# The eviction of a gate table from PSUM, walked in another order

## The chip, the cores and the metric

The kernel runs on one core of a Trainium2 chip. The metric is the device time of one execution in microseconds (us), the median of three runs. The core has five engines that run side by side, each in its own program order: TensorE (PE in the rows; PEld are its weight loads), VectorE (DVE), ScalarE (ACT), GpSimd (POOL) and SyncE (SP), which issues most transfers. Matmuls write to PSUM, a memory of eight banks with 512 float32 for each of 128 partitions; VectorE and ScalarE take results out of it ("evict" them) to SBUF, the large on-chip memory.

## What is computed

The reference is a trunk of two layers over 512 tokens of width 1024: attention heads of four kinds, then a layer of 16,384 small experts of which each token picks 128 (16 for each of 8 heads). The change lies in that second part:

```
def peer_ffn(h, w_q, sub_k1, sub_k2, u, v):
    q = (hf @ w_q).reshape(t, PEER_HEADS, 2, PEER_QUERY_DIM // 2)
    ...
    eid = jnp.take_along_axis(cid, top_j, axis=-1)
    gate = jax.nn.softmax(top_s, axis=-1)
    ...
        act = jax.nn.gelu(jnp.einsum('cd,ced->ce', hc, u[ec]).astype(jnp.float32))
        w = (gc * act).astype(hc.dtype)
        return jnp.einsum('ce,ced->cd', w, v[ec])
```

An expert's number is 128 times its first half plus its second half, two numbers below 128.

## The kernel before

Tokens lie in four tiles of 128. For three of them (384 tokens) the kernel doesn't gather experts but multiplies with all of them: 128 blocks of 128 experts go through TensorE, first with `u` (`u_mm`, line 1381, whose result `u_act` puts through gelu into `act`), later with `v`. Between the two each block's `act` is multiplied with the gates, which are zero for experts that a token didn't pick. For that a **gate table** is built in each layer, one gate for each token and each of the 16,384 experts. The fourth tile's tokens gather their experts with indirect transfers by GpSimd.

The table is built from pairs of one-hot rows, eight tokens (a "block" `b`) at a time, 48 blocks in a layer:

- `g_ones` (line 1657, VectorE) writes the one-hot rows of both halves of the expert numbers, tile `o`.
- `g_scale` (line 1664) multiplies those of the first half with the gates, in a high and a low part, tile `og`: the high part on VectorE (line 1675), the low part on VectorE or as eight small instructions on ScalarE (line 1673).
- `g_mm` (line 1677) multiplies them on TensorE. A bank of PSUM then holds four tokens of 128 second halves each, `(t a)` in its columns, with the first halves on the partitions. Each bank takes eight matmuls of 128 columns.
- `g_out` (line 1685) evicts that bank on ScalarE into the staging tile `gs`, `[128, 128, TG]`, whose last axis holds the tokens of a group of `TG` = 32: in `gs` the 128 second halves of one token lie 32 floats (128 bytes) apart, and neighbouring tokens lie next to each other. Four tokens fill 4 of the 32 places, eight evictions fill a tile.
- `g_put` (line 1691, SyncE) writes a full `gs` tile, 2 MB, to `gdram` in DRAM. There are 12 in a layer, and two `gs` tiles.

Later `gq_load` (line 1828) reads four blocks of experts at a time back, `w_mul` multiplies them into `act`, and `w_split` feeds the products with `v`.

The order of the work is set when the kernel is built, by the class `Plan` (line 100): it takes pieces of work with rough lengths and due times and lists them, and each engine runs its list in that order. For the eviction it reckons with 0.49 us on ScalarE (line 1724), for the scaling with 0.602 on VectorE or 2.4 on ScalarE, for the one-hot rows with 1.135. The first products with `u` are put between the pieces of the table (lines 1737 to 1749); the last four of those that go ahead are held until the table's last matmul is out. Buffers: three of `o`, two of `og`, six banks of PSUM.

The names in the rows below: `o<-iota,iT` are the one-hot rows, `og<-o,gT` and `og<-o,gL` the scaling on VectorE and on ScalarE, `psa<-og,o` the matmuls of the table, `gs<-psa` the eviction, `psb<-bh,uh` (and two more) the products with `u`, `gq<-gdram` the table's way back. The fourth token tile's expert numbers (`oh`, `pr`, `cid`, `ts`) are worked out on VectorE meanwhile.

Of the kernel before, what the change touches and what calls it, by code (L numbers as in the profile page):

```python
# [16 lines left out]
AF = mybir.ActivationFunctionType  # L17
# [25 lines left out]
GSC = 2.0 ** 14  # L43
# [12 lines left out]
# the chunks of w_in: for each run of columns the size of the rotated heads, the tile, the place in it, the width  # L56
# [22 lines left out]
def pairs(n):  # L79
    """the runs (first row, rows, columns) of pairs of ranks that can be among the n largest sums"""  # L80
    runs = []
    for k in range(n):
        w = n // (k + 1)
        if runs and runs[-1][2] == w:
            runs[-1][1] += 1
        else:
            runs.append([k, 1, w])
    return runs
# [11 lines left out]
class Plan:  # L100
    """an order for pieces of work, from rough lengths: each starts as soon as its inputs, buffers and engine allow, the most urgent first"""
# [28 lines left out]
    def holds(self, eng):  # L130
        """what a piece of work holds: its engine, and the way to SBUF that vector operations on two tiles (W) share with Pool"""
        return {"W": ("V", "port"), "G": ("G", "port") if LOCK else ("G",)}.get(eng, (eng,))
# [19 lines left out]
def trunk(ctx: ExitStack, tc: tile.TileContext, I, out):  # L152
    nc = tc.nc
    V, S, G, PE, SY = nc.vector, nc.scalar, nc.gpsimd, nc.tensor, nc.sync
# [79 lines left out]
    def ada_sum(j, acc, c):  # L234
        """sums over the rows, down the partitions or along the free axis"""
        ps = bank("b")
        if j in COL:
            for c in range(KD):
                PE.matmul(ps[:, c:c + 1], lhsT=acc[:, c * 128:(c + 1) * 128], rhs=ones[:, 0:1], start=True, stop=True)
        else:  # L240
            PE.matmul(ps[0:1], lhsT=ones[:, 0:1], rhs=acc[:, c * 512:(c + 1) * 512], start=True, stop=True)
        return ps
# [34 lines left out]
    def norm_cols(l, which):  # L277
        """the scale and the shift of a norm, once they are asked for"""
        g = small.tile([128, KD], F32, name="ng", bufs=2)
        SY.dma_start(g, I["norm_g"][l, which])  # L280
        got = []

        def cols():
            if not got:
                m = mods[l]
                gs = small.tile([128, KD], F32, name="ngs", bufs=2)
                V.scalar_tensor_tensor(gs, m["col"][:, 2 * which + 1], 1.0, g, op0=ALU.add, op1=ALU.mult)
                got.extend((gs, m["col"][:, 2 * which]))
            return got
        return cols  # L290

    def norm_parts(x, cols, pool, put, tag, nv=NV):
        """normed and modulated rows of one token tile, transposed, four chunks at a time: four steps"""
        xn = pool.tile([128, D], F32, name="xn", tag="xn", bufs=2)
        ps = {}

        ss = small.tile([128, 1], F32, name="nss")

        def squares():
            S.activation(xn, x, AF.Square, accum_out=ss)  # L300

        def scaled():
            rs = small.tile([128, 1], F32, name="nrs")
            rsqrt_mean(rs, ss, D)
            V.tensor_scalar(xn, x, rs, None, op0=ALU.mult)

        def turn(half):
            ps[half] = bank(tag)
            for k in range(4):
                PE.transpose(ps[half][:, k * 128:(k + 1) * 128], xn[:, (4 * half + k) * 128:(4 * half + k + 1) * 128], ident)  # L310

        def modulated(half):
            gs, sh = cols()
            h = pool.tile([128, 4, 128], F32, name="hf", tag="hf", bufs=3)
            for k in range(4):
                c = 4 * half + k
                if k < 4 - nv:
                    S.activation(h[:, k], ps[half][:, k * 128:(k + 1) * 128], AF.Identity, scale=gs[:, c:c + 1], bias=sh[:, c:c + 1])
                else:
                    V.tensor_scalar(h[:, k], ps[half][:, k * 128:(k + 1) * 128], gs[:, c:c + 1], sh[:, c:c + 1], op0=ALU.mult, op1=ALU.add)  # L320
            put(half, h)
        return squares, scaled, turn, modulated
# [39 lines left out]
    def rows_out(l):  # L362
        """what is done with each tile of rows that leaves layer l - 1"""
        if l == L:
# [19 lines left out]
            def halves(i, x, pool):  # L384
                """the same for a tile of rows that comes in two halves"""
# [28 lines left out]
    def early_mc(nat_):  # L414
        """the place of the first chunk's columns until the tiles they lie in are needed"""
        flat = {q: nat_[q].rearrange("p a b c -> p (a b c)") for q in ("dq", "dk")}
        return [flat["dq"][:, 384 * i:384 * i + 384] for i in range(3)] + [flat["dk"][:, :384]]

    def first_chunk(nat_, hh, hl):
        """the products with the first chunk of w_in, for a tile of rows and some of the inner blocks"""  # L420
        ps = {}

        def part(i, ks, wh, wl):
            if ks[0] == 0:
                ps[i] = bank("a")
            tsl = slice(i * 128, (i + 1) * 128)
            for k in ks:
                mm3(ps[i][:, :384], hh[:, k, tsl], hl[:, k, tsl], wh[:, k], wl[:, k], k == 0, k == KD - 1)
            if ks[-1] == KD - 1:
                S.activation(early_mc(nat_)[i], ps[i][:, :384], AF.Copy)  # L430
        return part

    class Room:
        """a pool over parts of tiles that nothing else needs yet"""
# [8 lines left out]
    def begin(O, RST, tp, more, hh, hl):  # L443
        """the modulation of the first norm, and what is done around the first chunk of w_in"""
# [39 lines left out]
    def w_in_phase(l, raw_, hh, hl, tp, pa, RST, O):  # L484
        """the products with w_in; what the heads need is made ready behind the chunk that follows"""
# [5 lines left out]
        def stack(dst, lo, hi, src, key):  # L491
            """one head transposed twice; the lower copy of a query, or a third and a fourth of a key, reduced to what float32r leaves"""
# [162 lines left out]
    for l in range(L):  # L655
        lam_init = 0.8 - 0.6 * math.exp(-0.3 * l)
        rcm, hcm, nat, hh, hl = state
        with tc.tile_pool(name=f"O{l}", bufs=1) as po_:
            O = po_.tile([128, KD, T], F32, name="O")
            # attention sub-layer  # L660
# [107 lines left out]
        # expert sub-layer  # L768
# [6 lines left out]
def attention(ctx, nc, tc, I, l, lam_init, st, O, RST, tp, small, bank, rope, nhalf, ca, ident, blk, rcm, right, ada):  # L775
# [20 lines left out]
    # differential lambda  # L796
# [18 lines left out]
    # NSA gates  # L815
# [22 lines left out]
    class Group:  # L838
        """four maps of one tile of tokens: scores, exponentials with the maximum taken off, sums, weights, sums of the values"""
# [56 lines left out]
        def plan(self, ready, before=None):  # L896
            """all of it; what the sums of the values go on from, if they do, is before"""
# [266 lines left out]
    def diff_prep(d, side, step, eng=None):  # L1164
        """differential queries of four maps one below the other, each with zeros in the place of the others, and the keys"""
# [26 lines left out]
    def mla_up(i, step):  # L1192
        """queries, keys and values of the latent heads"""
# [56 lines left out]
    # NSA  # L1250
# [59 lines left out]
    # more of the modulation  # L1310
# [45 lines left out]
def peer(nc, tc, I, l, xd, fh, fl, h3, closing, q0, w012, both, wq_mm, right, hp, up, small, bank, mm3, iota128, pos, ident, dram, grow, ada, more, rows_out):  # L1356
# [7 lines left out]
    # experts whose first product is kept in DRAM until the second one  # L1364
# [28 lines left out]
    with tc.tile_pool(name=f"Q{l}", bufs=1) as qp:  # L1393
# [25 lines left out]
        def wq_part(h, half, eng):  # L1419
            """one of the two parts of four blocks of rows of a head's w_q"""  # L1420
# [14 lines left out]
        def wq_late(h, c):  # L1435
            """the second half of the rows of the first two heads"""
            wq_mm(q0[2 * h + c], w[h], c, slice(256, 512), fh, fl)
# [10 lines left out]
        def key_mm(h, i):  # L1448
            """scores of the keys of one head"""
# [8 lines left out]
        def top16(rows, n):  # L1458
            """the 16 largest of each row and their places, with the rows in turn"""
# [12 lines left out]
        def key_best(h, i):  # L1472
            """the 16 largest of either half"""
# [13 lines left out]
        def pick(h):  # L1487
            """the sums of the 16 largest of the halves that can be among the 16 largest"""
# [9 lines left out]
        # the products with w_q and the best keys of each head  # L1498
# [5 lines left out]
        for h in range(8):  # L1504
# [25 lines left out]
            for i in range(NT):  # L1530
                # the rows that come late last
# [15 lines left out]
        def turn_over():  # L1547
            """the room of w_q goes to the sums of the first experts and to the gate table"""
# [19 lines left out]
        if True:  # L1568
# [9 lines left out]
            def ids(i, q, eng):  # L1578
                """numbers of the experts of the candidates for four slots of each head"""
# [55 lines left out]
            def turn(i):  # L1635
                """the halves of the expert numbers and the gates, slots on the partitions"""
# [20 lines left out]
            def g_ones(b):  # L1657
                """one-hot rows of the halves of the expert numbers of eight tokens"""
# [5 lines left out]
            def g_scale(b, q, eng):  # L1664
                """the first of them times the gates, in two parts"""
# [19 lines left out]
            def g_out(j):  # L1685
# [3 lines left out]
                S.activation(gst[tg][:, :, 4 * t4:4 * t4 + 4].rearrange("p a t -> p t a"), gps.pop(j).rearrange("p (t a) -> p t a", t=4), AF.Copy, scale=1 / GSC)  # L1689
# [4 lines left out]
            # the numbers and gates of the experts  # L1694
# [19 lines left out]
            # the gate table  # L1714
# [13 lines left out]
            # what can be done ahead of the sums over all experts  # L1728
# [77 lines left out]
    def g_weights():  # L1806
        """gate weights of the next eight slots, once a few later dot products are behind them"""
# [11 lines left out]
    with tc.tile_pool(name=f"D{l}", bufs=1) as dp, ExitStack() as order:  # L1819
# [57 lines left out]
        # made ready for the last products and for what follows them: what the steps before leave room for  # L1877
# [78 lines left out]
        with tc.tile_pool(name=f"X{l}", bufs=1) as xp:  # L1956
# [26 lines left out]
            # a tile of rows at a time, so that what follows can start on the first  # L1983
# [161 lines left out]
```

## Time and profile before

| | |
|---|---|
| time, median of 3 runs | 3389.96 us (3385.28 to 3396.86) |
| profiled execution, span from first to last instruction | 3387.4 us |
| TensorE busy | 3202.0 us, 95% |
| VectorE busy | 2593.0 us, 77% |
| ScalarE busy | 1542.2 us, 46% |
| evictions of the gate table (line 1689) | 192, 194.9 us |
| mean granted TensorE clock | 0.964 of full |

Busy time is the time in which an engine works on an instruction; neighbouring instructions of one engine overlap at their ends, so the step from one start to the next can be shorter than one instruction lasts. An average over the span says little: a layer has stages with different limits, and the windows below cut the building of the table out of it. The chain of work that ended last is followed back from the last instruction, at each step to what released it.

### The profile page before, as it was taken

The numbers are of one execution on the slowest core, as the hardware profiler recorded it, in microseconds if no ns is written. First come the engines' busy times: TensorE is split into PE (matmuls) and PEld (weight loads), VectorE is DVE, ScalarE is ACT, GpSimd is POOL, SyncE is SP. The second block draws the span as 40 slices with busy tenths as digits, with TensorE's granted clock in tenths as the row PEclk, the third lists the DMA queues.
The fourth block names the chain that finished last, engine by engine and source line by source line (L and its number), as shares of the span: only waits on it lengthen the run. The fifth ranks groups of instructions, "written<-read, shape, count | busy, mean of one in ns | idle before, by whom it ended". The sixth has DMA issues, their size and how long they took to land.

```text
span 3387.4 us, 48323 instructions
## 1 busy us (share of the span) xinstructions
PE 3202.0 (95%) x17540; PEld 2820.4 (83%) x17540; DVE 2593.0 (77%) x5460; ACT 1542.2 (46%) x2799; POOL 988.0 (29%) x756
## 2 busy tenths in 40 slices
PE   6988999979999999999999889999799999999998
PEld 6955879968989999998898568798699899999987
DVE  6487699867878888786665877988587788777766
ACT  3376526883333333333344764278633333333333
POOL 1254120003434343341023532100143344444400
PEclk9988999979999999999998999998799999999999
DMA  6223404458989998896632233044588899999954
GB/s 219 66 92 101 158 26 144 174 210 313 346 308 339 337 335 328 326 351 231 200 117 74 90 125 139 28 154 180 221 320 326 315 341 325 324 324 325 323 186 166
DMA packets 291342, 762.76 MB, mean 225 GB/s; under 512 B 23832, under 2 KB 130968, under 8 KB 285984
## 3 DMA queue, kind: packets, MB, share of 16 engines
q1 hardware_dynamic: 217376, 491.22, 42.0%
q0 software_dynamic: 73728, 268.47, 21.5%
q8 instruction: 137, 2.24, 0.3%
q14 instruction: 101, 0.83, 0.1%
HBM read 700.86 MB, written 58.74 MB: 224 GB/s over the span
## 4 chain that ended last, share of the span: by engine, by line
PE 76%; DVE 13%; ACT 6%; DMA 2%; issue 1%; POOL 0%; SPq 0%; DVEq 0%; POOLq 0%; ACTq 0%
PE psa L204 13%; PE psa L205 13%; PE psa L203 13%; PE psb L203 9%; PE psb L205 9%; PE psb L204 9%; ACT gs L1689 3%; PE psa L1683 2%; PE psa L851 2%; ACT og L1673 2%; DMA gq<-gdram 1%; PE psa L884 1%; DVE s L1466 1%; DVE ki L1464 1%; DVE ki L1470 1%
## 5 line engine op out<-in xcount | busy, mean ns | idle before, releaser
L203 PE MATMUL psb<-bh,uh 128*128 128x384 f32 x2048 | 692.0, 338 | 3.4 <-ACT act L1392 2.8
L205 PE MATMUL psb<-bh,ul 128*128 128x384 f32 x2048 | 688.7, 336 | 3.1 <-DVE ul L1379 3.1
L204 PE MATMUL psb<-bl,uh 128*128 128x384 f32 x2048 | 687.2, 336 | 0.0
L203 PE MATMUL psa<-vh,wdh 128*128 128x512 f32 x1512 | 590.3, 390 | 17.2 <-ACT wdh L1844 17.2
L205 PE MATMUL psa<-vh,wdl 128*128 128x512 f32 x1512 | 593.5, 393 | 0.0
L204 PE MATMUL psa<-vl,wdh 128*128 128x512 f32 x1512 | 593.3, 392 | 0.0
L1779 POOL DMA_INDIRECT gt<-in_peer_u,eid x256 | 338.2, 1321 | 727.9 <-DVE gt L1799 234.8
L1844 ACT ACTIVATE wdh<-act 128x384 fp32r<-128x384 f32 x252 | 132.1, 524 | 866.2 <-PE psa L204 637.3
L1779 POOL DMA_INDIRECT gt<-in_peer_v,eid x256 | 323.0, 1262 | 426.5 <-DVE a L1804 197.9
L203 PEld LDWEIGHTS psb<-bh,uh 128*128 128x128 f32 x2048 | 386.4, 189 | 13.8 <-ACT act L1392 4.0
L204 PEld LDWEIGHTS psb<-bl,uh 128*128 128x128 f32 x2048 | 385.9, 188 | 7.3
L205 PEld LDWEIGHTS psb<-bh,ul 128*128 128x128 f32 x2048 | 385.3, 188 | 4.8 <-DVE ul L1379 4.4
L1379 DVE TENSOR_TENSOR ul<-ur,uh 128x1024 fp32r<-128x1024 f32 x246 | 301.6, 1226 | 98.4 <-ACT uh L1376 84.9
L1845 DVE TENSOR_TENSOR wdl<-act,wdh 128x384 fp32r<-128x384 f32 x252 | 140.9, 559 | 285.4 <-ACT wdh L1844 274.5
L203 PEld LDWEIGHTS psa<-vh,wdh 128*128 128x128 f32 x1512 | 285.0, 189 | 73.0 <-ACT wdh L1844 17.8
L205 PEld LDWEIGHTS psa<-vh,wdl 128*128 128x128 f32 x1512 | 284.8, 188 | 60.0
L1856 DVE TENSOR_TENSOR vl<-vr,vh 128x1024 fp32r<-128x1024 f32 x252 | 307.7, 1221 | 34.1 <-ACT vh L1853 22.8
L204 PEld LDWEIGHTS psa<-vl,wdh 128*128 128x128 f32 x1512 | 284.8, 188 | 55.8
L1804 DVE SCALAR_TENSOR_TENSOR a<-gt,w,a 128x1024 f32<-128x1024 f32 x254 | 325.5, 1282 | 0.8
L1799 DVE SCALAR_TENSOR_TENSOR gt<-gt,h 128x1024 f32<-128x1024 f32 x256 | 310.8, 1220 | 0.0
L1376 ACT ACTIVATE uh<-ur 128x1024 fp32r<-128x1024 f32 x256 | 268.5, 1049 | 75.4 <-PE psb L204 63.6
L1392 ACT ACTIVATE act<-psb 128x384 f32<-128x384 f32 x256 | 126.8, 495 | 334.6 <-PE psb L205 334.5
(386 smaller groups left out, 5565.5 us busy)
## 6 DMA issues: line engine op xcount, KB each, us to landing
ur<-in_peer_uT SPq DMA_DIRECT2D x256, 512.0 KB
vr<-in_peer_v SPq DMA_DIRECT2D x256, 512.0 KB
gdram<-gs SPq DMA_DIRECT2D x24, 2048.0 KB
gq<-gdram SPq DMA_DIRECT2D x64, 768.0 KB
aw<-in_ada_w SPq DMA_DIRECT2D x58, 512.0 KB
gt<-in_ada_w SPq DMA_DIRECT2D x32, 512.0 KB
wr<-in_w_q SPq DMA_DIRECT2D x14, 1024.0 KB
wr<-in_w_out SPq DMA_DIRECT2D x16, 512.0 KB
```

Source lines behind the costliest of these rows:

```text
L203: PE.matmul(ps, lhsT=wh, rhs=mh, start=first, stop=False)
L204: PE.matmul(ps, lhsT=wh, rhs=ml, start=False, stop=False)
L205: PE.matmul(ps, lhsT=wl, rhs=mh, start=False, stop=last)
L1376: S.activation(uspl[e][0], uraw[e], AF.Copy)
L1379: eng.tensor_sub(uspl[e][1], uraw.pop(e), uspl[e][0])
L1392: S.activation(acts[e], ups.pop(e)[:, :384], AF.Gelu_apprx_tanh)
L1779: G.indirect_dma_start(out=t, out_offset=None, in_=I["peer_u" if kind == "u" else "peer_v"], in_offset=bass.IndirectOffsetOnAxis(ap=eid3[: ...
L1799: V.scalar_tensor_tensor(t, t, 1.0, h3, op0=ALU.mult, op1=ALU.mult, accum_out=d3[:, s:s + 1])
L1804: V.scalar_tensor_tensor(a3, t, w3[:, s:s + 1], a3, op0=ALU.mult, op1=ALU.add)
L1844: S.activation(wh, w, AF.Copy)
L1845: V.tensor_sub(wl, w, wh)
L1856: V.tensor_sub(vspl[e][1], vraw.pop(e), vspl[e][0])
```

## The change

One line of `g_out` is written in another way. The instruction stays one ACTIVATE on ScalarE that copies 128 x 512 float32 with a scale. Before, both sides were walked token by token (`p t a`): 128 second halves of a token, then the next token. Now both are walked second half by second half (`p a t`): the four tokens of one second half, then the next second half. The numbers and the places that they go to are the same. (The rest of the diff drops comments and docstrings.)

```
-                S.activation(gst[tg][:, :, 4 * t4:4 * t4 + 4].rearrange("p a t -> p t a"), gps.pop(j).rearrange("p (t a) -> p t a", t=4), AF.Copy, scale=1 / GSC)
+                S.activation(gst[tg][:, :, 4 * t4:4 * t4 + 4], gps.pop(j).rearrange("p (t a) -> p a t", t=4), AF.Copy, scale=1 / GSC)
```

`Plan` is told the same 0.49 us as before, so every engine's list keeps its order; on ScalarE the rows of the eviction alone read differently. This is the piece of ScalarE's list at the end of the first layer's table, the last three scalings on ScalarE (`og`) and the evictions (`gs`) around them:

```order
-L1673 ACTIVATE og<-o,gL 128x128 x8
-L1689 ACTIVATE gs<-psa 128x4x128 x4
-L1673 ACTIVATE og<-o,gL 128x128 x8
-L1689 ACTIVATE gs<-psa 128x4x128
-L1673 ACTIVATE og<-o,gL 128x128 x8
-L1689 ACTIVATE gs<-psa 128x4x128 x7
```

```order
+L1673 ACTIVATE og<-o,gL 128x128 x8
+L1689 ACTIVATE gs<-psa 128x128x4 x4
+L1673 ACTIVATE og<-o,gL 128x128 x8
+L1689 ACTIVATE gs<-psa 128x128x4
+L1673 ACTIVATE og<-o,gL 128x128 x8
+L1689 ACTIVATE gs<-psa 128x128x4 x7
```

Nothing moved: the same rows stand in the same places, with the eviction's free axes as 128x4 instead of 4x128.

## Rows read from the trace of the kernel before

**Rows 1.** The page, part 4: chain that ended last, by engine, by line.

```profile
PE 76%; DVE 13%; ACT 6%; DMA 2%; issue 1%; POOL 0%; SPq 0%; DVEq 0%; POOLq 0%; ACTq 0%
PE psa L204 13%; PE psa L205 13%; PE psa L203 13%; PE psb L203 9%; PE psb L205 9%; PE psb L204 9%; ACT gs L1689 3%; PE psa L1683 2%; PE psa L851 2%; ACT og L1673 2%; DMA gq<-gdram 1%; PE psa L884 1%; DVE s L1466 1%; DVE ki L1464 1%; DVE ki L1470 1%
```

**Rows 2.** Windows: length; PE, PEld, DVE, ACT, POOL busy (count); clock, DMA share, GB/s.

```profile
567.00:580.00 13.00, 11.91 (x85) 11.21 (x83) 11.35 (x14) 13.00 (x27) 0.00 (x0) 1.00 0.52 202
580.00:655.00 75.00, 75.00 (x504) 72.77 (x503) 63.36 (x112) 65.05 (x114) 5.75 (x2) 1.00 0.52 190
667.14:679.40 12.26, 8.99 (x64) 7.31 (x64) 11.33 (x15) 12.26 (x26) 0.00 (x0) 0.64 0.44 171
679.40:728.38 48.98, 35.28 (x256) 29.30 (x256) 39.20 (x61) 48.98 (x97) 0.00 (x0) 0.59 0.41 172
728.38:741.06 12.68, 11.25 (x73) 9.91 (x73) 6.87 (x17) 12.68 (x26) 0.00 (x0) 0.73 0.40 167
741.06:767.50 26.44, 17.02 (x96) 16.06 (x94) 5.37 (x5) 5.02 (x7) 6.84 (x6) 0.93 0.96 353
...
2354.60:2403.64 49.04, 35.30 (x256) 29.31 (x256) 39.20 (x61) 49.04 (x97) 0.00 (x0) 0.62 0.41 172
```

**Rows 3.** The same, of line 1689 alone: length, ACT busy (count), clock, DMA.

```profile
580.00:655.00 75.00, 28.33 (x27) 1.00 0.52 190
```

**Rows 4.** Timeline, one cycle: start, length, engine, group, [idle before, releaser].

```profile
703.80 0.69 DVE L1675 TENSOR_TENSOR og<-o,gT 128x1024 f16<-128x1024 f16 x1
703.86 2.66 ACT L1673 ACTIVATE og<-o,gL 128x128 f16<-128x128 f16 x8
704.40 0.78 DVE L1584 TENSOR_TENSOR cid<-ifl 128x128 int16<-128x128 int16 x7
704.44 4.41 PE L1683 MATMUL psa<-og,o 128*128 128x128 f16 x32 [1.70 <-ACT og L1673]
705.10 0.69 DVE L1675 TENSOR_TENSOR og<-o,gT 128x1024 f16<-128x1024 f16 x1
706.26 3.92 ACT L1689 ACTIVATE gs<-psa 128x512 f32<-128x512 f32 x4
706.88 0.69 DVE L1675 TENSOR_TENSOR og<-o,gT 128x1024 f16<-128x1024 f16 x1 [1.10 <-PE psa L1683]
707.49 2.52 DVE L1661 TENSOR_TENSOR o<-iota,iT 128x2048 f16<-128x2048 f16 x2
709.99 2.66 ACT L1673 ACTIVATE og<-o,gL 128x128 f16<-128x128 f16 x8
```

**Rows 5.** Groups by line and shape: count, busy us, mean ns, idle before.

```profile
L1689 ACT ACTIVATE gs<-psa 128x512 f32<-128x512 f32 x192 | 194.9, 1142 | 7.7 <-PE psa L1683 6.3
L790 ACT ACTIVATE PT<-psa 128x512 f32<-128x512 f32 x64 | 36.6, 591 | 17.5 <-PE psa L884 17.3
L1646 DVE CAST iT<-psa 128x256 f16<-128x256 f32 x6 | 2.5, 418 | 0.0
L792 DVE COPY PT<-psa 128x256 f32<-128x256 f32 x4 | 1.7, 422 | 0.0
L565 DVE TENSOR_TENSOR x<-x,posk 128x992 f32<-128x992 f32 x2 | 3.7, 1871 | 0.0
L1379 DVE TENSOR_TENSOR ul<-ur,uh 128x1024 fp32r<-128x1024 f32 x246 | 301.6, 1226 | 98.4 <-ACT uh L1376 84.9 <-issue 13.3
```

**Rows 6.** Timeline, three straight evictions on ScalarE in a row.

```profile
222.46 1.55 ACT L790 ACTIVATE PT<-psa 128x512 f32<-128x512 f32 x3
```

**Rows 7.** Timeline, the end of the first layer's table.

```profile
732.34 4.30 PE L1683 MATMUL psa<-og,o 128*128 128x128 f16 x31 [0.84 <-ACT og L1673]
734.16 6.87 ACT L1689 ACTIVATE gs<-psa 128x512 f32<-128x512 f32 x7
```

**Rows 8.** The chain that ended last, what follows it: start, length, what.

```profile
741.06 7.25 DMA gdram<-gs
749.71 17.20 DMA gq<-gdram
```

## The prediction

> **What bounds the kernel now.** I read the chain of work that ended last first: TensorE holds 76% of it, yet the eviction at line 1689 has 3% of its own and the scaling at line 1673 another 2% [rows 1]. Of some 3387 us, 5% is 170 us in which ScalarE, not TensorE, sets the pace. The windows by stage show where. While the first expert products are mixed in (580 to 655 us), TensorE is busy for 75.00 of 75.00 us and ScalarE for 65.05: there ScalarE hides. From 667.14 to 728.38 us it is the other way round: ScalarE is busy for 12.26 of 12.26 and 48.98 of 48.98 us, VectorE for 11.33 + 39.20, TensorE for 8.99 + 35.28 [rows 2]. The second layer repeats it [rows 2]. Matmuls are idle there and the granted clock falls to 0.59 of full speed, near the lower level of 1.2 GHz, for lack of work and not as a cause.
>
> The timeline shows what ScalarE does in it: a cycle of eight scalings and four evictions [rows 4]. From 703.86 to 706.26 (2.40 us) the scalings of an odd block run, from 706.26 to 709.99 (3.73 us) four evictions: 6.13 us a cycle, with no gap. TensorE works 4.41 us of it and waits 1.70 for ScalarE; VectorE waits 1.10 for TensorE. So an eviction costs 0.93 us of the path in this stage, although one lasts 1142 ns (neighbours overlap).
>
> **The one edit: what an eviction costs afterwards.** It stays one instruction of 128x512; there are 96 in each layer, in the same place on every queue, so no wait is added and nothing is moved past another queue. What changes is the walk. Before, PSUM is read straight through and each element is written 128 bytes from the last one in SBUF. Afterwards four neighbouring elements (16 bytes) are written in a run and then 128 bytes are hopped, but each element is read 512 bytes from the last one in PSUM.
>
> What the write costs is in the trace: the same 128x512 from PSUM, straight on both sides, lasts 591 ns against 1142 [rows 5], and three in a row take 1.55 us, a step of (1.55 - 0.59) / 2 = 0.48 us [rows 6]. So the scattered write doubles the eviction. That runs of four are enough to lose the penalty is shown on VectorE: the copy at line 1646 writes runs of four halves out of PSUM and lasts 418 ns for 256 columns, the straight copy 422 [rows 5].
>
> What the scattered read from PSUM costs no row shows. Every read of PSUM in this kernel is straight. Lower bound: nothing, a step of 0.48 us. A gain below that has no source, since 0.48 us is already the straight copy. Upper bound: a read on VectorE, from SBUF, with 64 bytes between elements lasts 1871 ns for 992 elements, where a straight one lasts 1226 for 1024 [rows 5]: 1.89 - 1.20 = 0.69 ns an element, 0.35 us for 512. Added to an eviction that kept its whole write penalty that is 1.49 us, a step of 1.28. I take the lower end: the row with scattered reads is of the other memory and another engine, and the only accesses to PSUM in the trace keep ScalarE's full pace. This is the weakest step, and the rivals below hang on it.
>
> The Trainium skill (Advanced Engine Details and Errata, section Memory Cachelines) says that SBUF wants two hits in each 16-byte line for full speed and PSUM two in each 8-byte line, and that patterns that aren't contiguous there slow matmuls. Its SBUF half agrees with 1142 against 591 ns; its PSUM half, read onto an eviction, speaks against the change, since each read would open a line of its own, and the eviction would stay near 1142 ns and the time near 3390 us. No run here shows that half.
>
> **The long stretch, 667.14 to 728.38 us.** It is ten cycles long (two irregular, eight regular): 61.24 us. ScalarE alone would now need 2.40 + 4 x 0.48 = 4.32 us a cycle. What is late next is VectorE. Its busy time over the stretch is 11.33 + 39.20 = 50.53 us, 5.05 a cycle [rows 2], in order: two one-hot tiles, three scalings, and a piece of the last token tile's expert numbers [rows 4]. Its wait for TensorE goes, I reckon: the scaling that waits needs the products of the odd block before. TensorE needs 4.41 us for both blocks, and VectorE comes to that scaling 5.05 us after the last one, so the products are done some 0.6 us earlier. I take VectorE's busy time and 0.5 us for joints: 51 us, a saving of 10.2 us. As ScalarE isn't the bound any more, this term needs only an eviction step under (5.05 - 2.40) / 4 = 0.66 us, not 0.48.
>
> **The end of the table, 728.38 to 741.06 us.** The last products end at 732.34 + 4.30 = 736.64 us; ScalarE has seven evictions standing then and ends at 734.16 + 6.87 = 741.03 [rows 7]. With steps of 0.48 it keeps up with the products and ends one eviction after them, near 736.64 + 0.1 + 0.6 = 737.3: a saving of 3.7 us. On it hangs the last write of the table to DRAM (7.25 us) and the first read back (17.20 us) [rows 8], which start when the last eviction ends; the loads around them are released by the same work. TensorE is busy for 17.02 of the 26.44 us from there to the first product that needs the table [rows 2], so there is room for them to come 3.7 us sooner: 9.4 us idle.
>
> **The front.** Between 567 and 580 us ScalarE is full (13.00 of 13.00) and TensorE idles 1.09 us [rows 2]: I count 1 us. From 580 to 655 nothing: TensorE is the cover. Were it gone, the 27 evictions in it [rows 3] would count too. In the short stretch from 655 to 667 I count 0.5 us, an estimate from the three evictions that stand before its last scaling (3 x 0.45 = 1.35), most of which TensorE's products hide.
>
> **The sum.** A layer: 10.2 + 3.7 + 1 + 0.5 = 15.4 us; both: 30.8. The loop over the experts that follows waits for nothing else and starts that much sooner. The profiled execution has a span of 3387.4 us, 2.6 below the median of 3389.96; so 3356.6 for the span and about 3359 for the median: 0.9% faster. About 0.3% (10 us) is what a measurement of this kernel can tell from no change.
>
> **Rivals.**
> *The penalty only changes sides.* One access in each pair is still scattered, now the read. If a scattered read of PSUM holds ScalarE as a scattered write to SBUF does, the step stays 0.93, the cycle 6.13, the time 3390 us. For it: the hop grows from 128 to 512 bytes, and [rows 5] has a scattered read that costs on VectorE. Against it: that is SBUF. 15%.
> *A part of it.* With a step of 0.75 us ScalarE stays the bound: 2.40 + 3.00 = 5.40 a cycle, a saving of 7.3 us over ten, and 7 x 0.18 = 1.3 at the end, 0.7 in front: 9.3 a layer, 3371 us. 8%.
> *Slower: the read costs more than the write did.* ScalarE has no slack in the long stretch, so it turns slower from the first nanosecond that a step is over 0.93. At the upper bound of 1.28 us: 40 evictions x 0.35 = 14 us there, 7 x 0.35 = 2.5 at the end. In the covered stretch 65.05 + 27 x 0.35 = 74.5 of 75 us still hides [rows 2, 3]; of the 20 or so other evictions (7 us) I count 4.5, since ScalarE is already full from 567 to 580. 21 us a layer, 3432 us. Against it: both bounds must be at their worst together. 9%.
> *The saving stops at VectorE.* If its own waits for TensorE don't shrink, the cycle is 5.05 + 1.10 = 6.15 and only the end is won: 5.2 us a layer, 3380 us. For it: it is the fuller of the two remaining engines. Against it: the wait is for products that themselves wait 1.70 us for ScalarE. Two cycles in between can fall to 4.4 us, TensorE's own need. 4%.
>
> **How the numbers follow.** My forecast 64%, a part 8%, stops at VectorE 4%, the same 15%, slower 9%. Faster by over 0.3%: 64 + 8 and half of the 4 = 74%; within 0.3%: 15 + 2 = 17%; slower 9%. The forecast alone is 3351 to 3368: 17 us a layer if all joints vanish, 13.5 if a cycle is 5.3, and 5 us for the scatter (three runs lie between 3385.28 and 3396.86). Eight in ten needs the unchanged case too, so the range is 3351 to 3394; it leaves out the slower case and a little beside.
>
> **What would show it.** The group of line 1689 with about 600 ns instead of 1142: the read is free. Near 1142: the first rival. In the long stretch ScalarE is no longer full, VectorE is over 95% busy and a cycle takes about 5.1 us. The last eviction of each layer ends within 1 us of the last product of the table, and the write to DRAM starts 15 us sooner in the first layer and 31 in the second. The stretch from 580 to 655 us keeps its length. Wrong would be a shorter eviction with cycles still at 6.1 us, or a gain that the loop over the experts gives back.

## The result, and the profile after

The changed kernel takes 3354.86 us (median of 4 runs, 3348.74 to 3358.83). The kernel before, run beside it, took 3392.47 us. The ratio is 0.9898, with a 95% interval from 0.9877 to 0.9919: about 1.0% faster. The forecast was 3359 us, in a range from 3351 to 3394. The profiled execution spans 3356.9 us, against 3387.4 before: 30.5 us less, where the sum of the prediction had 30.8.

First the page of the changed kernel, part 1 (busy time, share of the span, instructions), and part 4 (the chain of work that ended last), to be laid beside [rows 1]:

```profile
PE 3196.3 (95%) x17540; PEld 2823.5 (84%) x17540; DVE 2588.2 (77%) x5460; ACT 1468.2 (44%) x2799; POOL 990.0 (29%) x756
...
PE 79%; DVE 16%; DMA 2%; ACT 2%; issue 1%; POOL 0%; SPq 0%; DVEq 0%; POOLq 0%; ACTq 0%
PE psa L204 13%; PE psa L205 13%; PE psa L203 13%; PE psb L203 10%; PE psb L205 10%; PE psb L204 10%; PE psa L1683 4%; PE psa L851 2%; PE psa L884 1%; DVE o L1661 1%; DMA gq<-gdram 1%; DVE s L1466 1%; DVE og L1675 1%; DVE ki L1464 1%; DVE ki L1470 1%
```

ScalarE did as many instructions as before in 74.0 us less (1468.2 against 1542.2). The eviction at line 1689, 3% of the chain before, is gone from it, and so is ScalarE's scaling at line 1673; VectorE's share rose from 13 to 16%, and its one-hot rows (line 1661) and scaling (line 1675) stand there now. TensorE's matmuls of the table (line 1683) rose too, from 2 to 4%: the chain now goes back and forth between VectorE and them. That the bound of the stage has moved to VectorE, as forecast, is what experiments 3 and 4 test.

The group of the eviction (count, busy us, mean ns, idle time before and what ended it), which answers to the first row of [rows 5]:

```profile
L1689 ACT ACTIVATE gs<-psa 128x512 f32<-128x512 f32 x192 | 111.4, 613 | 35.7 <-PE psa L1683 33.8
```

1142 ns have become 613. The idle time in front of it rose from 7.7 to 35.7 us: ScalarE now waits for TensorE's products, where they waited for it.

The windows by stage (length; busy time of PE, PEld, DVE, ACT, POOL with counts; clock, DMA share, GB/s). The first two are the first two stretches of [rows 2]; the next three run between the same pieces of work as the others there, which come earlier now: the ten cycles, the end of the table, and the way to the first product that needs it. The last is the ten cycles of the second layer.

```profile
567.00:580.00 13.00, 12.49 (x89) 12.06 (x87) 10.76 (x14) 11.10 (x28) 0.00 (x0) 0.91 0.55 216
580.00:655.00 75.00, 75.00 (x499) 73.00 (x498) 63.73 (x112) 53.69 (x112) 5.74 (x2) 0.99 0.52 190
667.60:716.09 48.49, 40.20 (x307) 34.95 (x306) 45.91 (x70) 45.92 (x122) 0.00 (x0) 0.64 0.53 217
716.09:727.01 10.92, 8.66 (x66) 8.08 (x66) 10.39 (x20) 9.23 (x25) 0.00 (x0) 0.66 0.46 194
727.01:754.37 27.36, 20.96 (x119) 20.64 (x117) 5.64 (x7) 5.27 (x8) 6.53 (x6) 0.94 0.92 338
...
2326.25:2374.74 48.49, 40.22 (x307) 34.98 (x306) 45.91 (x70) 45.91 (x121) 0.00 (x0) 0.61 0.53 218
```

From 580 to 655 us ScalarE lost 11.4 us of work (65.05 to 53.69) and nothing came of it: TensorE is busy for 75.00 of 75.00 us both times. The gain is in the ten cycles, 61.24 us before (667.14 to 728.38) and 48.49 now: 12.75 us. ScalarE and VectorE are each busy for 95% of them, so this row doesn't tell which of the two sets the pace. The end of the table went from 12.65 us (728.38 to the end of the last eviction, 741.03) to 10.92.

One cycle in the timeline, to be laid beside [rows 4] (start, length, engine, group; in brackets the wait before it and what ended it):

```profile
690.50 2.70 ACT L1673 ACTIVATE og<-o,gL 128x128 f16<-128x128 f16 x8
690.99 4.15 PE L1683 MATMUL psa<-og,o 128*128 128x128 f16 x32 [0.70 <-DVE og L1675]
690.99 3.52 PEld L1683 LDWEIGHTS <-o 128*128 128x128 f16 x30 [0.86 <-issue]
691.46 1.22 DVE L1661 TENSOR_TENSOR o<-iota,iT 128x2048 f16<-128x2048 f16 x1
692.94 1.64 ACT L1689 ACTIVATE gs<-psa 128x512 f32<-128x512 f32 x3
692.96 1.23 DVE L1661 TENSOR_TENSOR o<-iota,iT 128x2048 f16<-128x2048 f16 x1 [0.28 <-PE psa L1683]
694.10 0.69 DVE L1675 TENSOR_TENSOR og<-o,gT 128x1024 f16<-128x1024 f16 x1
694.70 0.74 DVE L1593 TENSOR_TENSOR oh<-tf,pos 128x1120 f16<-128x1120 f16 x1
694.84 0.60 ACT L1689 ACTIVATE gs<-psa 128x512 f32<-128x512 f32 x1 [0.25 <-PE psa L1683]
```

TensorE waits 0.70 us for VectorE's scaling (before: 1.70 for ScalarE's), ScalarE waits 0.25 for TensorE, and VectorE waits 0.28 for TensorE to let go of a buffer of `o`. The three evictions last 1.64 us, a step of (1.64 - 0.60) / 2 = 0.52 us, where it was 0.93. From 680.90 to 716.09 us there are seven such cycles, 5.03 us each on average (4.6 to 5.4, since VectorE's piece of the expert numbers differs), against 6.13 in the same seven before. First the window before, then the one after:

```profile
685.50:728.38 42.88, 30.89 (x224) 25.64 (x224) 34.57 (x51) 42.88 (x85) 0.00 (x0) 0.60 0.35 148
680.90:716.09 35.19, 28.82 (x224) 25.62 (x224) 33.16 (x49) 32.62 (x86) 0.00 (x0) 0.68 0.46 195
```

### The profile page after: what moved, and what is told of

Read it like the earlier page. It is cut to its first block, busy times and chain, and to the rows that moved or that the text cites. A ratio compares the mean times of both kernels' runs of the same rounds, so it can differ in the third digit from the quotient of the medians.

```text
span 3356.9 us, 48323 instructions
## 1 busy us (share of the span) xinstructions
PE 3196.3 (95%) x17540; PEld 2823.5 (84%) x17540; DVE 2588.2 (77%) x5460; ACT 1468.2 (44%) x2799; POOL 990.0 (29%) x756
## 4 chain that ended last, share of the span: by engine, by line
PE 79%; DVE 16%; DMA 2%; ACT 2%; issue 1%; POOL 0%; SPq 0%; DVEq 0%; POOLq 0%; ACTq 0%
PE psa L204 13%; PE psa L205 13%; PE psa L203 13%; PE psb L203 10%; PE psb L205 10%; PE psb L204 10%; PE psa L1683 4%; PE psa L851 2%; PE psa L884 1%; DVE o L1661 1%; DMA gq<-gdram 1%; DVE s L1466 1%; DVE og L1675 1%; DVE ki L1464 1%; DVE ki L1470 1%
```

## Experiments

Two questions were open: why the eviction became shorter, and whether ScalarE set the cycle before and VectorE does now.

**1. The scattered read alone.** The new kernel reads PSUM with hops of 512 bytes. Here both sides are walked straight, so the table's numbers land in other places:

```
-  S.activation(gst[tg][:, :, 4 * t4:4 * t4 + 4], gps.pop(j).rearrange("p (t a) -> p a t", t=4), ...)
+  S.activation(gst[tg].rearrange("p a t -> p (a t)")[:, 512 * t4:512 * t4 + 512], gps.pop(j), ...)
```

> The eviction reads PSUM straight and writes 512 floats straight into the staging tile (so the table's entries land in wrong places; the amount of data stays). Theory (a read with 512 bytes between elements costs ScalarE next to nothing, and the long stretch is set by VectorE and TensorE): the eviction lasts about 590 ns against 613 of the changed kernel, and the time stays at 3355 us, within 0.2%. Rival (the scattered read still costs a good part): the eviction falls well below the changed kernel's, and with ScalarE on the path the time falls by 10 us or more.

Measured: 3354.27 us, ratio 0.9879 (0.9862 to 0.9895). The group of the eviction in its profile:

```profile
L1689 ACT ACTIVATE gs<-psa 128x512 f32<-128x512 f32 x192 | 111.3, 610 | 35.8 <-PE psa L1683 33.9
```

610 ns straight, 613 with the scattered read: on ScalarE the hops through PSUM cost nothing that can be measured.

**2. Both sides scattered.** Of each token first every other second half is walked, then the ones left out: the read of PSUM has 8 bytes between elements and the write to SBUF 256, so neither side has two neighbours in a row.

```
+  S.activation(gst[tg][:, :, 4 * t4:4 * t4 + 4].rearrange("p (b r) t -> p t r b", r=2),
+               gps.pop(j).rearrange("p (t b r) -> p t r b", t=4, r=2), ...)
```

> The eviction walks every second expert index, token by token: the read has 8 bytes between elements, the write 256. No run of two elements on either side. Theory (only the write to SBUF has a penalty): about 1140 ns as in the kernel before, and 3390 us. Rival (a scattered read of PSUM has a penalty of its own, which adds): 1.3 to 1.5 us for an eviction, and 3410 to 3435 us.

Measured: 3390.83 us, ratio 0.9999 (0.9987 to 1.0012).

```profile
L1689 ACT ACTIVATE gs<-psa 128x512 f32<-128x512 f32 x192 | 192.1, 1132 | 7.8 <-PE psa L1683 6.4
```

1132 ns, as the kernel before (1142) with its straight read. So the whole difference is on the side of the write, and a read with hops of 8 bytes adds nothing to it. Whether such a read would cost something that the slow write covers, this run can't tell; for hops of 512 bytes the first experiment has shown that it doesn't.

**3. More work for VectorE, in the changed kernel.** VectorE's first scaling of every even block is done twice.

```
                 else:
                     eng.tensor_mul(h[:, q], o, bc(g[:, :, None, :], [128, 2, 128, 4]))
+                    if q == 0 and b % 2 == 0:
+                        eng.tensor_mul(h[:, q], o, bc(g[:, :, None, :], [128, 2, 128, 4]))
```

> The changed kernel, with VectorE's first scaling of each even block done twice (0.61 us of VectorE more in a cycle, the result is the same). Theory (VectorE with the products it waits for now sets the cycle): a cycle of the long stretch goes from 5.03 to about 5.6 us, 6 us a layer, 3367 us. Rival (ScalarE or TensorE sets it still): 5.0 us and 3355 us.

Measured: 3376.33 us, ratio 0.9947 (0.9931 to 0.9964), some 20 us more than the changed kernel. The windows of the seven cycles and of the end of the table, the group of the repeated scaling, and its shortest, median and longest duration in ns:

```profile
680.90:721.58 40.68, 28.77 (x224) 25.68 (x224) 38.40 (x62) 33.81 (x86) 0.00 (x0) 0.67 0.37 156
721.58:733.94 12.36, 8.95 (x67) 8.20 (x68) 11.80 (x22) 9.62 (x25) 0.00 (x0) 0.64 0.41 172
...
L1677 DVE TENSOR_TENSOR og<-o,gT 128x1024 f16<-128x1024 f16 x46 | 40.2, 873 | 1.6
...
L1677 DVE TENSOR_TENSOR og<-o,gT x46: 691/692/2782, 553.4 to 2396.5; 128x1024 f16<-128x1024 f16 x46
```

A cycle takes 5.81 us instead of 5.03, and VectorE's busy time in one rose from 33.16 / 7 = 4.74 to 5.49 us: what VectorE gets to do is paid in full. That VectorE sets the pace holds. The size was missed: in these cycles the repeat lasts 0.69 us like the other scalings, but it starts 0.72 us after the one that it repeats, where the instruction behind that one started after 0.60, so that it adds some 0.73 us and not 0.61. And the end of the table pays as well, 12.36 us against 10.92. (The mean of 873 ns comes from four repeats of 2.77 us, none of them in the ten cycles or at the end.)

**4. The same in the kernel before.**

> The same doubled scaling in the kernel before. Theory (ScalarE sets the cycle there, VectorE has 1.2 us to spare): the cycle stays 6.12 us and the time 3390 us, within 0.2%. Rival (VectorE was the bound all along, and the walk helped it in some way): 12 us more.

Measured: 3393.3 us, ratio 0.9997 (0.9983 to 1.0011). Its seven cycles:

```profile
687.26:730.11 42.85, 31.05 (x224) 25.57 (x224) 40.08 (x58) 42.85 (x85) 0.00 (x0) 0.58 0.35 148
```

42.85 / 7 = 6.12 us a cycle, as without the repeats; ScalarE is busy for all of it, and VectorE's 5.5 us more (40.08 against 34.57) lie in what were its waits. The same work is free in the one kernel and costs 20 us in the other: the bound did change hands.

**5. Runs of two.** To see what the write wants, the runs in SBUF are cut from four floats to two.

```
+  S.activation(gst[tg][:, :, 4 * t4:4 * t4 + 4].rearrange("p a (u t) -> p u a t", t=2),
+               gps.pop(j).rearrange("p (u t a) -> p u a t", u=2, t=2), ...)
```

> The eviction of the changed kernel, but with two tokens inside, then the 128 expert indices, then the two pairs: SBUF gets runs of two floats (8 bytes) and then a hop of 128 bytes. If what costs is every hop to a far place in SBUF, half of the hops are left, and the eviction lasts half way between the two kernels, about (1142 + 613) / 2 = 880 ns. If two neighbours are enough to keep ScalarE at its full pace, it lasts about 613 ns as with runs of four, and the time is that of the changed kernel, about 3355 us. If runs of two do nothing, 1142 ns and 3390 us.

**6. Two in the same 16 bytes, not side by side.**

```
+  S.activation(gst[tg][:, :, 4 * t4:4 * t4 + 4].rearrange("p a (v u) -> p u a v", u=2),
+               gps.pop(j).rearrange("p (v u a) -> p u a v", v=2, u=2), ...)
```

> As the run with pairs, but the two elements that follow one another are written 8 bytes apart instead of side by side: both lie in the same 16 bytes of SBUF, but they are not neighbours. If what counts is that neighbours are written side by side, every element is a hop of its own and the eviction lasts about 1142 ns (3390 us). If what counts is that both lie close together, within 16 bytes, it lasts as long as the run with pairs, whatever that is.

**7. The same, with the tile moved by 8 bytes.**

```
-  gst[tg] = dp.tile([128, 128, TG], F32, name="gs", tag="gs", bufs=GL[4])
+  gst[tg] = dp.tile([128, 128 * TG + 4], F32, name="gs", tag="gs", bufs=GL[4])[:, 2:2 + 128 * TG].rearrange("p (a t) -> p a t", t=TG)
```

> The kernel of the run that writes two elements 8 bytes apart, with the whole tile gs moved up by 8 bytes: the two elements are still 8 bytes apart and everything else is the same, but now one lies in the upper half of one 16-byte line and the other in the lower half of the next. If what counts is two hits in the same 16-byte line, every write opens a line of its own again: about 1142 ns an eviction, and the time of the kernel before, about 3390 us. If what counts is the distance alone, 649 ns and about 3350 us, as without the move. If lines are 32 bytes wide, half of the pairs stay within one, and the evictions fall into two kinds, near 649 and near 1142 ns.

Measured, a single time each: 3346.84 us for the runs of two, 3351.1 for two in the same 16 bytes (3387.71 before, beside them), and 3387.95 with the tile moved (3387.67 before). The group of the eviction in the profile of each, in this order:

```profile
L1689 ACT ACTIVATE gs<-psa 128x512 f32<-128x512 f32 x192 | 118.2, 650 | 31.4 <-PE psa L1683 28.9
```

```profile
L1689 ACT ACTIVATE gs<-psa 128x512 f32<-128x512 f32 x192 | 118.1, 649 | 31.4 <-PE psa L1683 29.0
```

```profile
L1689 ACT ACTIVATE gs<-psa 128x512 f32<-128x512 f32 x192 | 188.9, 1096 | 7.9 <-PE psa L1683 6.5
```

Two at a time are nearly as good as four (650 against 613 ns, far from the 880 of a cost for each hop), and they needn't be neighbours (649). But the same two, 8 bytes apart as before, cost 1096 ns as soon as the border of a 16-byte piece lies between them. So neither the run nor the distance counts, but how many consecutive writes fall into one aligned 16-byte line; with two nearly all of the cost is gone. All 192 evictions of the last run lie between 1037 and 1202 ns, none near 650: with lines of 32 bytes half of the pairs would have stayed inside one. A move of the tile that leaves the pairs inside their lines wasn't run; but in the runs of two half of the pairs begin 8 bytes into a line, and cost nothing for it. The Trainium skill (Advanced Engine Details and Errata, section Memory Cachelines) has this rule for SBUF, 16-byte lines and two hits in each, and the three runs agree with it, but for the 37 ns between two and four. Its PSUM half, 8-byte lines and patterns that aren't contiguous slowing matmuls, doesn't carry over to an eviction by ScalarE: 613 against 610 ns in the first experiment.

**8. The eviction in four pieces.** To lift the eviction step towards the prediction's threshold of 0.66 us:

```
+  ps = gps.pop(j).rearrange("p (t a) -> p a t", t=4)
+  for c in range(0, 128, 32):
+      S.activation(gst[tg][:, c:c + 32, 4 * t4:4 * t4 + 4], ps[:, c:c + 32], AF.Copy, scale=1 / GSC)
```

> The changed kernel with each eviction cut into four instructions of 128x128, each with the same runs of four in SBUF: the same elements, three more starts of an instruction on ScalarE. It raises the eviction step on ScalarE from 0.52 us to an estimated 0.7 to 0.8, at or just above the threshold of 0.66 us at which the prediction lets ScalarE become the bound of the cycle again. If VectorE sets the cycle (theory), four evictions more at 0.2 us use up the 0.7 us in which ScalarE now waits in a cycle, so the cycle stays between 5.03 and 5.3 us and the whole costs at most about 5 us more than the changed kernel (3355 to 3360 us). If every ns of the eviction is on the path (rival), four times 0.2 us are added to each cycle (5.8 us) and the whole is some 15 to 20 us slower than the changed kernel (3370 to 3375).

Measured: 3357.69 us, ratio 0.9912 (0.989 to 0.9934). The windows of the same seven cycles and of all ten:

```profile
677.98:713.61 35.63, 30.81 (x221) 25.02 (x219) 33.66 (x50) 35.63 (x173) 0.00 (x0) 0.55 0.44 186
662.84:713.61 50.77, 43.88 (x313) 35.55 (x311) 48.27 (x73) 50.77 (x242) 0.00 (x0) 0.53 0.50 208
```

The seven take 5.09 us each, the ten 50.77 us against 48.49, and ScalarE is full again: 35.63 of 35.63 and 50.77 of 50.77. With 2.40 us for the scalings an eviction now takes about (5.09 - 2.40) / 4 = 0.67 us, so this kernel stands about on the threshold, where ScalarE and VectorE need the same: its cycles are nearly even (5.0 to 5.2 us in the last eight), where those of the changed kernel go from 4.5 to 5.4 with VectorE's work. The 40 evictions, 0.15 us longer each, are 6 us more of ScalarE's work; 2.3 us came of it in the ten cycles: the rest was slack. The expectation of at most 5 us in the whole held (2.8 us between the medians), and that every ns of the eviction is on the path is out.

**9. Four buffers of `o`.** This takes away the 0.28 us that VectorE waits in a cycle, with every engine's list in the same order.

```
-  o = oo[b] = dp.tile([128, 4, 128, 4], F16, name="o", tag="o", bufs=GL[0])
+  o = oo[b] = dp.tile([128, 4, 128, 4], F16, name="o", tag="o", bufs=4)
```

> The changed kernel with four buffers instead of three for the one-hot tile o, in the same order on every engine. In the changed kernel VectorE waits 0.28 us a cycle for TensorE's products to free a buffer of o. If VectorE's own work is what sets the cycle and this wait is what keeps it from its full pace, the cycle goes from 5.03 to about 4.75 us: 10 cycles x 0.28 = 2.8 us in each layer, about 5.6 us in all (3349 us). If TensorE or ScalarE is late next at the same place, or the waiting only moves to the other buffers (og has two), the cycle and the time stay (3355 us, within 2).

Measured: 3352.32 us (3339.81 to 3361.55), ratio 0.9892 (0.9869 to 0.9915). The windows of seven cycles and of all ten:

```profile
680.76:713.27 32.51, 27.44 (x224) 26.16 (x223) 32.48 (x49) 31.82 (x85) 0.00 (x0) 0.59 0.50 211
667.42:713.27 45.85, 38.79 (x307) 35.71 (x306) 45.62 (x71) 45.16 (x121) 0.00 (x0) 0.57 0.56 230
```

In the trace it does what it should: 4.64 us a cycle instead of 5.03, 2.6 us less in the ten cycles, VectorE busy for 32.48 of 32.51 us. By that some 5 us of the whole, 0.16%, should be won. The times don't tell it from the changed kernel (0.9892 against 0.9898, with intervals of 0.4%), so that it is faster is not shown. VectorE and ScalarE (31.82) are both nearly full there, so a further buffer has little left to win in it. The granted clock of TensorE was 0.57 in these ten cycles and 0.64 in those of the changed kernel, which are longer: a higher clock isn't what makes a cycle short here.

## Why the prediction was right, point by point

**The cost of the eviction.** Forecast: 1142 to about 600 ns, a step of 0.48 us; measured 613 and 0.52. The choice that was called the weakest step, to count the scattered read from PSUM at nothing, was right: 613 against 610 ns. It rested on no row of PSUM, so it was a choice rather than a reading, and in that it was lucky; experiment 1 is what shows it. The other half, that runs of four lose the whole penalty, was taken over from VectorE's copy [rows 5] and held; experiments 5 to 7 say why, and that two would nearly have done.

**The ten cycles.** VectorE became the bound, as forecast (experiments 3 and 4). The forecast of 5.05 us a cycle met 5.03 in the seven regular ones, but by two errors that cancelled: VectorE's busy time is 4.74 us there and not 5.05, and its wait for TensorE shrank from 1.10 to 0.28 us instead of going. The term as a whole came out too small, 10.2 forecast against 12.75 us. The sum let VectorE do 50.53 us of work in that stretch. It did 45.91, and more of it behind the stretch (below). The trace shows what moved. These are the windows of the ten cycles and of the end of the table with the one-hot rows alone (line 1661: length, VectorE's busy time, count; an instruction across a border counts in both), before and after:

```profile
667.14:728.38 61.24, 25.41 (x21) 0.60 0.41 172
728.38:741.06 12.68, 0.04 (x1) 0.73 0.40 167
...
667.60:716.09 48.49, 23.22 (x19) 0.64 0.53 217
716.09:727.01 10.92, 2.45 (x2) 0.66 0.46 194
```

Before, VectorE had all 48 tiles of one-hot rows ready by the end of the ten cycles; now two are left for the end of the table. With the scalings (line 1675) it is alike: 31 started in the ten cycles before, 28 now. So VectorE's lead over the others is smaller. That it had the lead because ScalarE was late, as far as the buffers of `o` and `og` let it, is my reading; no run tests that.

**The end of the table.** Forecast 3.7 us, measured 12.65 - 10.92 = 1.7. Here the same work comes back: VectorE is busy for 10.39 of 10.92 us, where it was 6.87 of 12.68. The mechanism was right, as the end of the table in the timeline shows beside [rows 7]:

```profile
724.45 1.93 PE L1683 MATMUL psa<-og,o 128*128 128x128 f16 x15 [1.23 <-DVE og L1675]
726.41 0.60 ACT L1689 ACTIVATE gs<-psa 128x512 f32<-128x512 f32 x1 [0.35 <-PE psa L1683]
```

The last eviction starts 0.03 us after the last product (724.45 + 1.93 = 726.38) and ends 0.6 us later, instead of 4.4 us after it. But the last products themselves wait for VectorE. The two terms together were forecast at 13.9 us and measured at 12.75 + 1.73 = 14.5.

**The front.** Forecast 1.5 us, measured 0.4 in the first layer: from the first eviction to the first of the ten cycles it was 667.14 - 550.78 = 116.4 us and is 667.60 - 551.62 = 116.0. But in the second layer it was 119.1 us and is 116.1, 3.0 less. The granted clock differs. The windows of the two layers before, of the two after, and of the first layer in experiment 1, whose evictions last as long as those of the changed kernel:

```profile
550.78:667.14 116.36, 114.61 (x783) 110.66 (x782) 96.69 (x167) 101.95 (x171) 5.75 (x2) 0.99 0.48 172
2223.00:2342.14 119.14, 117.40 (x783) 113.45 (x782) 96.83 (x167) 102.13 (x172) 5.74 (x2) 0.97 0.47 168
...
551.62:667.60 115.98, 114.96 (x782) 111.53 (x781) 96.09 (x166) 83.61 (x172) 5.74 (x2) 0.98 0.47 173
2210.14:2326.25 116.11, 115.09 (x782) 111.66 (x781) 96.22 (x166) 83.63 (x171) 5.74 (x2) 0.98 0.48 173
...
556.47:671.54 115.07, 114.04 (x782) 110.53 (x781) 96.08 (x166) 83.63 (x172) 5.73 (x2) 1.00 0.47 174
```

TensorE is busy for nearly all of each. From 567 to 580 us its granted clock was 1.00 before and 0.91 after, so the first layer shows less than the change gives there; in the second layer the lower clock was the one before (0.97 against 0.98), and it shows more. The mean of the two layers is 1.7 us, and the front of experiment 1 is 1.3 us shorter than the one before, at nearly the same clock (1.00 and 0.99). Why the clock fell where it did is not shown. So the forecast of 1.5 was near; that 1.09 us of TensorE's idle time from 567 to 580 us would go as a whole was too much, 0.51 stayed.

**What follows the table.** The last write to DRAM goes out 14.0 us sooner in the first layer (727.03 against 741.06; forecast 15), and the first product that needs the table is made ready 13.2 us sooner (754.37 against 767.53). In between, the chain took another way than in [rows 8]:

```profile
730.98 0.19 PE psb L204
731.17 0.02 issue
731.19 1.07 ACT uh L1376
732.26 0.02 issue
732.28 1.24 DVE ul L1379
733.52 0.02 issue
733.54 0.33 SPq L1372
...
735.49 18.26 DMA gq<-gdram
```

Before, the chain came to SyncE's read of the table through the table's last write (7.25 us). Now it comes through a held product with `u`, its ScalarE and VectorE steps and a load of `ur` (line 1372) that stands ahead of the read on SyncE's queue. The prediction had put that down as released by the same work. It held, with a near tie: 735.49 - 727.01 = 8.48 us from the last eviction to the read, against 749.71 - 741.03 = 8.68. The read itself took 18.26 us against 17.20 in these two executions, which is most of the 0.8 us that was lost on the way. In the second layer the last write goes out 2416.05 - 2385.69 = 30.4 us sooner (forecast 31), and the loop over the experts gave nothing back that shows behind it: 30.5 us in the span. That this is so near the forecast of 30.8 is partly luck. The parts add up to 0.4 + 12.75 + 1.73 = 14.9 us in the first layer and to some 17.5 in the second, 32.4 in all. Of that 0.8 us are missing since the first eviction starts later (551.62 against 550.78), and 1.2 go between the layers: the second layer's first eviction starts 2223.00 - 2210.14 = 12.9 us sooner.

**The threshold.** That 0.48 us isn't needed and anything under 0.66 does was right: experiment 8 stands at 0.67, where ScalarE is just full again, and costs 2.3 us in the ten cycles.

**The rivals.** That the penalty only changes sides, a part of it and a slower read all fell with 613 ns. That the saving stops at VectorE needed waits of VectorE that don't shrink; in the ten cycles they shrank by three quarters, from 61.24 - 50.53 = 10.7 to 48.49 - 45.91 = 2.6 us.

## What to carry to other kernels

When one side of a float32 copy must be scattered, let ScalarE scatter its read from PSUM and not its write to SBUF; for the write, put at least two consecutive elements into the same aligned 16 bytes. With two 8 bytes apart check where the tile begins, since an offset of 8 bytes took nearly the whole gain away. A cheaper instruction pays only in the stretch where its engine is the last to finish, and only down to the need of the next engine: of the 83.5 us that the evictions lost (194.9 to 111.4), 30.5 reached the end. To learn which engine that is, give one engine a known piece of extra work in both kernels: it was free in one and cost 20 us in the other.

## What the runs showed of the hardware that was not expected

- ScalarE reads PSUM with 512 bytes between elements as fast as straight: 613 and 610 ns for 128x512 float32.
- The cost of its write to SBUF goes by aligned 16-byte lines: 649 ns with two writes in a row to each line, 1096 when the same two lie in neighbouring lines, 613 with four.
- In experiment 3, all but four of the repeated scalings on VectorE last 0.69 us, and those four 2.77 us. Each of the four runs while GpSimd has a subtraction of its own (2.83 to 2.90 us, line 1379), of which there are two in each layer's table stage. No run takes GpSimd's away, so the cause isn't tested.
